# The heads' space in two pools, the first freed one head early, and the gates' token sums made in the last head

## The chip, the core and the metric

The kernel runs on one core of one Trainium2 chip. The metric is the device time of one execution in microseconds (us): the median of three executions before the change is 1059.69 us, the lowest 1058.46 us and the highest 1060.88 us. The engines are named as the profile names them: PE is TensorE (matrix products; PEld is its weight load), DVE is VectorE, ACT is ScalarE, POOL is GpSimd and SP is SyncE. SP issues the loads of the weights, POOL the transfers between the steps of the heads.

## The reference, cut to what matters

One decoder layer over 256 tokens (S) of width 2048 (D_MODEL), everything in float32. All four gate and channel products are slices of one projection `proj`:

```python
h = _rmsnorm(x, pre_norm_g)
proj = jnp.einsum('bsd,de->bse', h, w_in)
(q_a, c_kv, k_rope, z_mla, c_in, b_gate, c_gate, z_conv, g_mla, g_conv) = jnp.split(proj, cuts, axis=-1)
...
attn = _causal_mla_attention(q_nope, q_rope, k_nope, k_rope, v)
attn = attn.reshape(b, s, MLA_WIDTH) * jax.nn.silu(z_mla)
y_mla = jnp.einsum('bse,ed->bsd', attn, w_o_mla)
u = c_gate * c_in
u_pad = jnp.pad(u, ((0, 0), (CONV_K - 1, 0), (0, 0)))
conv = sum(conv_w[k] * u_pad[:, k:k + s] for k in range(CONV_K))
y_conv = jnp.einsum('bse,ed->bsd', b_gate * conv * jax.nn.silu(z_conv), w_o_conv)
merged = jax.nn.sigmoid(g_mla) * y_mla + jax.nn.sigmoid(g_conv) * y_conv
out = jnp.einsum('bsd,de->bse', merged, w_out)
x = x + _rmsnorm(out, post_norm_g)
```

There are 16 heads. `g_mla` and `g_conv` are the gates whose "token sums" the change moves.

## The kernel before

**Exact products from split halves.** Every float32 operand is split into a high part in the reduced format fp32r and a low part, the rest; a product is three matmuls (high by high, high by low, low by high) into one PSUM bank (`product`). A weight comes in units of 1 MB, numbered in one plan. SP loads unit n into a buffer `raw`, ACT copies it into `whi` (the high part) and DVE subtracts, `wlo = raw - whi` (`split_act`, line 262). There are three buffers each of `raw`, `whi` and `wlo`: unit n+3 is loaded into the buffer of unit n once both engines have split that unit, and is split into the buffers of unit n once PE has read them. `ahead` issues three loads ahead and splits one unit ahead of the one in use.

**Stages.** First the latent projections, then a loop over 16 heads, then four gate blocks (two gates, two halves of the width), then the two square projections and the output projection. In the loop every head h has four channel units (`channels(h, 0)` to `channels(h, 3)`: a quarter of the contraction each, into two banks `cv`), between which stand the scores of the head, `turn` (the softmax weights of the head before it, turned through DRAM: DVE writes `via`, POOL stores it to `far` and loads it back as `p`, ACT and DVE split it into `pt`) and `values` (their product with V, in the bank `o`). The scores of head 15 are made in head 14 already. The units of head 14 are 105 to 108, those of head 15 are 109 to 112. `channels_done` empties the two `cv` banks (`cv_w`, line 726). Every fourth head the gated convolution is made on DVE and POOL (`taps`: three shifted copies `mv` of `cv_f`, each multiplied by a row `cw` of the convolution's weights, which POOL loads, line 743; DVE's products are line 759). The last one, for t = 0, is issued at the end of head 14 and its products are made in head 15.

**The gate blocks.** Of the 16 blocks of a gate's contraction six are taken in three pairs with a scheme of seven products instead of eight, which needs sums of weights (`split_pair`, lines 204 to 220: `tf` from `raw`, `raw` changed in place, `thi` and `tlo` the halves of `tf`) and sums of tokens (`token_sums`, lines 891 to 906: from `x_both`, sums `xf`, then four tiles `xsf`, split into `xs`). The eight banks of a gate block are those that the heads used: two of tag `cv`, one `o`, one `st`, four `mm`. The first gate block begins with unit 113, a plain unit (four banks: `cv`, `st`, `cv`, `o`, in this order); then come unit 114, a pair, 115, plain, 116, a pair, and so on by turns. Only pairs need `xs`, `tf`, `thi` and `tlo`, of which there is one buffer each.

**Memory.** `bp` is the pool of the loop over heads: the latent tiles `qa`, `ckv` and `kr`, the mask, and all temporary tiles (`temp`, line 326). It is closed after the last head (line 867), and `sg` (the gates' results) and `d1` (the gate blocks' tiles, with `xs`, `tf`, `thi`, `tlo`) are opened behind it, in the space that it leaves. So the first tile of `d1` can be written once the last transfer or instruction that reads the tiles of `bp` at that place is done.

**What sets the order.** A scheduler puts the instructions of ACT, DVE, POOL and SP into the order of each engine's queue when the program is built; matmuls and the calls marked `keep_in_program_order` stay in the order of the code. Each queue is then worked off in that order: an instruction that waits holds all behind it.

Of the kernel before, what the change touches and what calls it, by code (L numbers as in the profile page):

```python
# [11 lines left out]
F32 = mybir.dt.float32  # L12
F32R = mybir.dt.float32r
I32 = mybir.dt.int32
AF = mybir.ActivationFunctionType
ALU = mybir.AluOpType
PSUM = bass.MemoryType.PSUM

P = 128
S = 256  # L20
NT = S // P
D = 2048
KD = D // P
H = 16
# [4 lines left out]
KR = R // P  # L29
# [9 lines left out]
LINE = 32  # L39
# [3 lines left out]
PAIRS = 3  # L43
STEP = 4
# [40 lines left out]
def tile_layer(ctx: ExitStack, tc: tile.TileContext, xw, x, pos, pvec, post_g, wc, wz, wcv, wkr, wqk, wqr, wv, cwr, wsq, wg, out):  # L85
    nc = tc.nc
# [36 lines left out]
    for h in range(H):  # L123
        g, second = divmod(h, HG)
# [176 lines left out]
    main = ctx.enter_context(ExitStack())  # L301
# [5 lines left out]
    cv_f = fp.tile([P, KD, S], F32, name="cv_f")  # L307
    bstack = main.enter_context(ExitStack())
    bp = bstack.enter_context(tc.tile_pool(name="bp", bufs=1, side="right"))
    qa = bp.tile([P, KR, 2 * S], F32R, name="qa")  # L310
    ckv = bp.tile([P, KR, 2 * S], F32R, name="ckv")
    kr = bp.tile([P, 2, S], F32R, name="kr")
    mask = bp.tile([P, 3 * P], F32, name="mask")
    nc.gpsimd.memset(mask[:, :], 0.0)
    for o in (0, 2 * P):
        make_causal_mask(nc, mask[:, o : o + P], mask_val=MASKED)
# [9 lines left out]
    def temp(name, shape=(P, S), dt=F32, bufs=2, tag=None):  # L326

        tag, n = tag or name.rstrip("0123456789_"), shape[-1]
        if n % LINE == 0:
            return bp.tile(list(shape), dt, name=name, tag=tag, bufs=bufs)  # L330
        return bp.tile([P, -(-n // LINE) * LINE], dt, name=name, tag=tag, bufs=bufs)[:, :n]


    def turned(src, via, n):
# [402 lines left out]
    def taps(j, t):  # L737
# [31 lines left out]
        join(u, u, parts[0], ALU.add)  # L769
        yield  # L770

    cv_w = bp.tile([P, NT, 512], F32, name="cv_w")
    tap, coming, ps_by_head = None, [], {}

# [3 lines left out]
    def score(h):  # L778
        ps_by_head[h], come = scores(h)
        coming.append(come)  # L780

    for h in range(H):
        v, at = divmod(h, HV)

        if at == 0:
            for i in range(4):
                if v == 0 and i == 1:

                    def turn_keys():
                        latent_turn("ckv", ckv, "kv_g", (("mm", 4), ("mm", 4)))  # L790
                        next(table_parts)

                    gates(v, i, turn_keys)
                else:
                    gates(v, i)
                if v == 0 and i == 0:
                    latent_turn("qa", qa, "q_g", (("st", 1), ("o", 1)))
                elif v == 0 and i == 2:
                    key_rope()
                elif v and i == 0:  # L800
                    arrive()
                    pt = turn(ps_by_head.pop(h - 1))
                elif v and i == 1:
                    values(h - 1, pt)
                    make("v", v)
                    next(tap)
                elif v and i == 2:
                    next(tap)
            gates_done(v)
        if h == 0:  # L810
            for i in first:
                make(*i)
            channels(h, 0)
        if h < H - 1:
            score(h)
        if h:
            channels(h, 0)
        if at == 0:
            coming.append(gates_turn(v, 0))
        else:  # L820
            pt = turn(ps_by_head.pop(h - 1))
        channels(h, 1)
        if at == 0:
            arrive()
            coming.append(gates_turn(v, 1))
        else:
            values(h - 1, pt)
        if h == H - 2:
            score(h + 1)

        if at == 2 or h == H - 1:
            next(tap)
        if at and h < H - 1:
            arrive()
        channels(h, 2)
        if at == 0:
            arrive()
            if v:
                coming.append(channels_join(v - 1, 0))
        if at == 2 or h == H - 1:  # L840
            next(tap)
        for i in made[h]:
            make(*i)
        if h == H - 1:
            pt = turn(ps_by_head.pop(h))
        channels(h, 3)
        if at == 0:
            while coming:
                arrive()
        if h == H - 2:  # L850
            arrive()
        if h == H - 1:
            values(h, pt)
        if at == 3:
            coming.append(channels_join(v, 1))
        if at == 1:
            tap = taps(v, 1)
            next(tap)
        elif at == 3 and h + 1 < H or h == H - 2:
            tap = taps(v, 0)  # L860
            next(tap)
# [3 lines left out]


    bstack.close()
    sgp = main.enter_context(tc.tile_pool(name="sgp", bufs=1))
    sg = sgp.tile([P, 2, NT, D], F32, name="sg")
    dstack = main.enter_context(ExitStack())  # L870
    d1 = dstack.enter_context(tc.tile_pool(name="d1", bufs=1))
    at_both = m_both = x_both

    def split_turned(src, both, c, t):
# [9 lines left out]
    def split_channels(i):  # L884

        j, t = divmod(i, NT)
        split_turned(cv_t[:, j, t, :], cv_both, j, t)

    xs = d1.tile([P, 4, PAIRS, 2, P], F32R, name="xs")

    def token_sums():


        both = x_both[:, :, :].bitcast(F32).rearrange("p (g k) c -> p g k c", k=STEP)[:, :2, :PAIRS]
        xf = d1.tile([P, 2, PAIRS, S], F32, name="xf", tag="tf", bufs=1)
        s = d1.tile([P, 4, PAIRS, P], F32, name="xsf", tag="thi", bufs=1)
        tt = nc.vector.tensor_tensor
        for g in range(2):
            tt(xf[:, g], both[:, g, :, :S], both[:, g, :, S:], op=ALU.add)
        a = [[xf[:, g, :, t * P : (t + 1) * P] for g in range(2)] for t in range(NT)]  # L900
        tt(s[:, 0], a[1][0], a[1][1], op=ALU.add)
        tt(s[:, 1], s[:, 0], a[0][0], op=ALU.subtract)
        tt(s[:, 2], a[0][0], a[1][0], op=ALU.subtract)
        tt(s[:, 3], a[0][1], s[:, 1], op=ALU.subtract)
        for i in range(4):
            split_act(xs[:, i, :, 0], xs[:, i, :, 1], s[:, i])

    def side(n, j):

# [11 lines left out]
    def gate_block(n, b, last):  # L921


        units, kinds = u_g[2 * n + b], gate_kinds()[n, b]
        ps = {m: bank(f"g{n}{b}_{m}", *TAGS[m]) for m in TAGS}
        begun = set()
        ends = {}
        for i, (kind, _) in enumerate(kinds):
            for m in TAGS if kind == "pair" else ():
                ends[m] = i  # L930
            for m in (2, 3, 4, 0) if kind == "whole" else ():
                ends[m] = i
        last_pair = max(i for i, (kind, _) in enumerate(kinds) if kind == "pair")

        def add_to(m, a, w, i, end):
            product(ps[m][:, :], a, w, m not in begun, end and ends[m] == i)
            begun.add(m)

        for i, (kind, ks) in enumerate(kinds):
            if last:  # L940
                for v in {6: (0, 1), 7: (2,)}.get(i, ()):
                    split_branch(v)
            if n == b == i == 0:
                token_sums()
            w = take(units[i])
            if kind == "pair":
                for m in TAGS:
                    if m:
                        add_to(m, side(m, ks[0]), w[m], i, True)
            else:  # L950
                for m, t, half in ((2, 0, 0), (3, 0, 1), (4, 1, 0), (0, 1, 1)):
                    for j, k in enumerate(ks):
                        a = [x_both[:, k, o + t * P : o + (t + 1) * P] for o in (0, S)]
                        add_to(m, a, w(2 * j + half, 512), i, j == len(ks) - 1)
            if i == last_pair:
                p1, p5 = wide("p1"), wide("p5")
                u = d1.tile([P, 3, 512], F32, name="u", tag="u", bufs=1)
                nc.scalar.activation(p1[:, :], ps[1][:, :], AF.Copy)
                nc.scalar.activation(p5[:, :], ps[5][:, :], AF.Copy)
                tt = nc.vector.tensor_tensor  # L960
                tt(u[:, 0], ps[6][:, :], p1[:, :], op=ALU.add)
                tt(u[:, 2], ps[7][:, :], u[:, 0], op=ALU.add)
                tt(u[:, :2], u[:, 0::2], p5[:, :].rearrange("p (o c) -> p o c", o=1).to_broadcast([P, 2, 512]), op=ALU.subtract)
        for m, t, half, other in ((2, 0, 0, p1[:, :]), (3, 0, 1, u[:, 0]), (4, 1, 0, u[:, 2]), (0, 1, 1, u[:, 1])):
            o = 1024 * b + 512 * half
            g = sg[:, n, t, o : o + 512]
            tt(g, ps[m][:, :], other, op=ALU.add)
            nc.scalar.activation(g, g, AF.Sigmoid, scale=r_col[:, t : t + 1])
# [30 lines left out]

    for c in range(4):  # L1000
        pss = tokens(c, 0, at_both)
        if c == 1:
            fstack.close()
        for t, m in enumerate(merged(0, c)):
            nc.vector.tensor_tensor(m, pss[t][:, :], m, op=ALU.mult)
    waiting = None
# [201 lines left out]
```

## Time and profile before

| | |
|---|---|
| median of three executions | 1059.69 us |
| the profiled execution's own time | 1061.09 us |
| its span in the profile | 1059.3 us |
| PE busy, share of the span | 1024.0 us, 97% |
| DVE busy | 742.5 us, 70% |
| ACT busy | 532.5 us, 50% |
| POOL busy | 180.3 us, 17% |
| mean granted clock of PE | 0.988 |

The profile is one execution with the hardware's own times. Its page gives the busy time of each engine, the span in 40 slices of 26.5 us, the chain of work that ended last (followed back from the last instruction, at each step to what released it) and the costliest groups of instructions. Further views list instructions in order of time, waits by what ended them, and busy time in chosen stretches. In a row of the timeline stand the start, the time (of all of "x2" together), the engine, the line, the operation, output and input tiles, and in brackets the idle time of the engine before it with what ended it. The span is 1.8 us shorter than the profiled execution's time, which is 1.4 us above the median.

### The profile page before, as it was taken

What the parts mean: (1) busy time and instruction counts of PE and PEld (TensorE: products, weight loads), DVE (VectorE), ACT (ScalarE), POOL (GpSimd) and SP (SyncE); (2) the same over time, 40 slices, a digit from 0 to 9 for tenths busy, and PEclk for the clock granted to TensorE, in tenths of its full rate; (3) what the DMA queues carried; (4) which work ended last, traced back from release to release, by engine and by line L of the source; (5) the groups of instructions that cost most, each with busy time, mean ns of one, the idle gap of its engine ahead of it and who ended that gap; (6) DMA issues with size and microseconds to landing.
All of it is one profiled execution on the core that took longest, in us unless ns stands there. A gap on an engine that the chain in (4) does not pass through costs nothing.

```text
span 1059.3 us, 12469 instructions
## 1 busy us (share of the span) xinstructions
PE 1024.0 (97%) x4658; PEld 851.8 (80%) x4658; DVE 742.5 (70%) x960; ACT 532.5 (50%) x675; POOL 180.3 (17%) x345
## 2 busy tenths in 40 slices
PE   9999999999999999999999839999999999999997
PEld 8887888888878888788888728888888888888885
DVE  7578769686687777777677579797976445666462
ACT  7756546455465455455555145555565333334451
POOL 7621220204202042112422210000000000232000
PEclk9999999999999999999999969999999999999999
DMA  8754766667666685656767536655555555677842
GB/s 339 299 188 176 254 221 210 219 222 277 193 230 214 214 296 182 232 208 238 267 230 231 173 113 203 216 200 214 186 211 198 194 187 186 238 250 252 321 159 79
DMA packets 41948, 231.00 MB, mean 218 GB/s; under 512 B 7520, under 2 KB 8224, under 8 KB 18976
## 3 DMA queue, kind: packets, MB, share of 16 engines
q1 hardware_dynamic: 29808, 197.54, 52.4%
q0 software_dynamic: 11648, 29.38, 9.2%
q10 hardware_dynamic: 432, 3.29, 0.7%
q8 instruction: 36, 0.59, 0.2%
q14 instruction: 24, 0.20, 0.0%
HBM read 214.48 MB, written 11.53 MB: 213 GB/s over the span
## 4 chain that ended last, share of the span: by engine, by line
PE 90%; DVE 4%; issue 2%; DMA 2%; ACT 1%; POOL 1%; DVEq 0%; POOLq 0%
PE cv L90 28%; PE sq L90 16%; PE g L90 15%; PE z L90 8%; PE out L90 8%; PE qa L90 2%; PE qn L90 2%; PE ckv L90 2%; PE kn L90 2%; DMA cw<-cwr_dram 2%; PE vv L90 2%; PE sc L90 1%; DVE wlo L264 1%; ACT whi L263 1%; PE o L90 1%
## 5 line engine op out<-in xcount | busy, mean ns | idle before, releaser
L264 DVE TENSOR_TENSOR wlo<-raw,whi 128x1024 fp32r<-128x1024 f32 (+2 forms) x290 | 423.4, 1484 | 224.7 <-ACT whi L263 223.8
L263 ACT ACTIVATE whi<-raw 128x1024 fp32r<-128x1024 f32 (+2 forms) x292 | 357.5, 1259 | 380.3 <-issue 120.5
L90 PE MATMUL cv<-whi,x_both 128*128 128x512 f32 x1024 | 323.4, 390 | 3.3 <-DVE cv_w L726 3.3
L90 PEld LDWEIGHTS cv<-whi,x_both 128*128 128x128 f32 x1024 | 192.3, 188 | 43.5 <-DVE cv_w L726 4.3
L90 PE MATMUL cv<-wlo,x_both 128*128 128x512 f32 x512 | 199.7, 390 | 0.0
L90 PE MATMUL g<-whi,x_both 128*128 128x512 f32 x368 | 119.8, 390 | 0.0
L90 PEld LDWEIGHTS cv<-wlo,x_both 128*128 128x128 f32 x512 | 96.2, 188 | 18.7
L90 PEld LDWEIGHTS g<-whi,x_both 128*128 128x128 f32 x368 | 69.4, 189 | 14.4
L90 PE MATMUL z<-whi,x_both 128*128 128x512 f32 x256 | 80.6, 390 | 0.0
L90 PE MATMUL sq<-whi,x_both 128*128 128x512 f32 x256 | 79.0, 389 | 0.0
L90 PE MATMUL sq<-whi,cv_both 128*128 128x512 f32 x256 | 78.9, 389 | 0.0
L90 PE MATMUL out<-whi,x_both 128*128 128x512 f32 x256 | 78.9, 389 | 0.0
L345 POOL DMA_DIRECT2D far<-sg x32 | 17.5, 553 | 330.4 <-DVE sg L1014 287.8
L345 POOL DMA_DIRECT2D far<-via x64 | 35.3, 559 | 225.2 <-DVE via L338 224.2
L90 PE MATMUL g<-wlo,x_both 128*128 128x512 f32 x184 | 71.8, 390 | 0.0
L90 PEld LDWEIGHTS z<-whi,x_both 128*128 128x128 f32 x256 | 48.1, 188 | 9.9
L90 PEld LDWEIGHTS sq<-whi,cv_both 128*128 128x128 f32 x256 | 48.0, 188 | 9.9
L90 PEld LDWEIGHTS out<-whi,x_both 128*128 128x128 f32 x256 | 48.0, 188 | 9.9
L90 PEld LDWEIGHTS sq<-whi,x_both 128*128 128x128 f32 x256 | 48.0, 188 | 9.9
L90 PE MATMUL z<-wlo,x_both 128*128 128x512 f32 x128 | 49.8, 389 | 0.0
L90 PE MATMUL sq<-wlo,x_both 128*128 128x512 f32 x128 | 49.8, 389 | 0.0
L90 PE MATMUL sq<-wlo,cv_both 128*128 128x512 f32 x128 | 49.8, 389 | 0.0
(243 smaller groups left out, 1325.3 us busy)
## 6 DMA issues: line engine op xcount, KB each, us to landing
raw<-wcv_dram SPq DMA_DIRECT2D x64, 1024.0 KB, 5.1
raw<-wsq_dram SPq DMA_DIRECT2D x48, 1024.0 KB, 4.8
raw<-wg_dram SPq DMA_DIRECT2D x32, 1024.0 KB, 4.8
raw<-wz_dram SPq DMA_DIRECT2D x16, 1024.0 KB, 4.8
raw<-wqk_dram SPq DMA_DIRECT2D x8, 1024.0 KB, 5.6
cw<-cwr_dram POOLq DMA_DIRECT2D x24, 256.0 KB, 7.2
raw<-wc_dram SPq DMA_DIRECT2D x4, 1024.0 KB, 9.9
raw<-wv_dram SPq DMA_DIRECT2D x4, 1024.0 KB, 5.6
```

What stands on the lines that cost most here:

```text
L90: return tc.keep_in_program_order(nc.tensor.matmul(*a, **kw))
L263: a = nc.scalar.activation(hi, src, AF.Copy)
L264: b = nc.vector.tensor_tensor(lo, src, hi.bitcast(F32), op=ALU.subtract)
L345: tc.keep_in_program_order(nc.gpsimd.dma_start(out=f[i], in_=m))
```

## The change

The pool `bp` becomes two. `ep` stands behind it on the same side and takes `qa`, `ckv`, `kr`, the mask and those temporary tiles whose tags belong to the norms, the rotary tables, the queries and the keys; `bp` keeps the rest (`p`, `via`, `pt`, `f`, `cw`, `mv`, V). `ep` is closed in head 14, after the scores of head 15 are issued, and `d1` with `xs` is opened there, in its space and in what was free beside it. `token_sums` is called in head 15 after `channels(15, 2)`, behind the `turn` of head 15, which moves up ahead of the second step of the convolution, instead of in the first gate block. `sg` moves to the side where `bp` was; the space of `at_f` and `cv_f` is no longer released in the first square projection. The instructions are the same ones, 4,647 matmuls in the same order, and the queues of POOL and SP hold the same DMAs in the same order; DVE's and ACT's queues are ordered anew around heads 14 and 15.

```diff
-    qa = bp.tile([P, KR, 2 * S], F32R, name="qa")
...
+    estack = main.enter_context(ExitStack())
+    ep = estack.enter_context(tc.tile_pool(name="ep", bufs=1, side="right"))
+    qa = ep.tile([P, KR, 2 * S], F32R, name="qa")
+    ckv = ep.tile([P, KR, 2 * S], F32R, name="ckv")
+    kr = ep.tile([P, 2, S], F32R, name="kr")
+    mask = ep.tile([P, 3 * P], F32, name="mask")
...
+        pool = ep if tag.startswith(("rms_", "ta_", "rp_", "qn_", "kn", "qr")) else bp
...
+    def token_sums(d1, xs):
+        both = x_both[:, :, :].bitcast(F32).rearrange("p (g k) c -> p g k c", k=STEP)[:, :2, :PAIRS]
+        xf = d1.tile([P, 2, PAIRS, S], F32, name="xf", tag="tf", bufs=1)
+        s = d1.tile([P, 4, PAIRS, P], F32, name="xsf", tag="thi", bufs=1)
...
+    dstack = main.enter_context(ExitStack())
+    def sums_space():
+        estack.close()
+        d1 = dstack.enter_context(tc.tile_pool(name="d1", bufs=1))
+        return d1, d1.tile([P, 4, PAIRS, 2, P], F32R, name="xs")
...
         if h == H - 2:
             score(h + 1)
+            d1, xs = sums_space()
...
+        if h == H - 1:
+            pt = turn(ps_by_head.pop(h))
+            token_sums(d1, xs)
         if at == 2 or h == H - 1:
             next(tap)
         for i in made[h]:
             make(*i)
-        if h == H - 1:
-            pt = turn(ps_by_head.pop(h))
...
-    sgp = main.enter_context(tc.tile_pool(name="sgp", bufs=1))
+    sgp = main.enter_context(tc.tile_pool(name="sgp", bufs=1, side="right"))
...
-            if n == b == i == 0:
-                token_sums()
...
-        if c == 1:
-            fstack.close()
```

Three places of DVE's queue show what moved (line numbers are those of the kernel that a row belongs to; a tile's first number, as in `wlo110`, is the unit's or the head's). The first is the softmax of head 15, issued in head 14, up to the turn of its weights (`via_5067` before, `via_5070` now). `mx`, `nb` and `rs` are its row maxima, their negatives and the reciprocal sums; `wlo110` is the low half of unit 110; `cv_w` empties the banks of head 14. Before the change:

```order
L633 TENSOR_REDUCE mx_5055<-p_5049 128x1 x2
L634 TENSOR_SCALAR nb_5058<-mx_5055 128x2
L641 RECIPROCAL rs_5057<-sm_5056 128x2
L644 TENSOR_SCALAR p_5049<-p_5049,rs_5057 128x128
L644 TENSOR_SCALAR p_5049<-p_5049,rs_5057 128x256
L338 STREAM_TRANSPOSE via_5067<-p_5049 128x3x4x32
L759 TENSOR_TENSOR mv1_4917<-mv1_4917,cw_4923 128x512
L759 TENSOR_TENSOR mv2_4920<-mv2_4920,cw_4925 128x512
L264 TENSOR_TENSOR wlo110_5166<-raw110_5114,whi110_5165 128x1024 x2
```

and after it, where `xf` (two instructions), `nb` and two of the four `xsf` stand just ahead of these rows, between `mx` and the first of them:

```order
L264 TENSOR_TENSOR wlo110_5174<-raw110_5122,whi110_5173 128x1024
L786 TENSOR_TENSOR xsf_5289<-xsf_5289,xf_5288 128x384
L264 TENSOR_TENSOR wlo110_5174<-raw110_5122,whi110_5173 128x1024
L644 RECIPROCAL rs_5060<-sm_5059 128x2
L788 TENSOR_TENSOR xsf_5289<-xf_5288,xsf_5289 128x384
L264 TENSOR_TENSOR xs_5081<-xsf_5289,xs_5081 128x3x128 x2
L729 SCALAR_TENSOR_TENSOR cv_w_617<-cv14_0_4964,r_both_105,cv_w_617 128x512
L647 TENSOR_SCALAR p_5052<-p_5052,rs_5060 128x128
L647 TENSOR_SCALAR p_5052<-p_5052,rs_5060 128x256
L264 TENSOR_TENSOR xs_5081<-xsf_5289,xs_5081 128x3x128 x2
L729 SCALAR_TENSOR_TENSOR cv_w_617<-cv14_1_4965,r_both_105,cv_w_617 128x512
L341 STREAM_TRANSPOSE via_5070<-p_5052 128x3x4x32
```

The token sums (`xf`, `xsf`, `xs`), unit 110 and both `cv_w` of head 14 now stand ahead of `via`; before, unit 110 and the two `cv_w` stood behind it and the sums from 29 rows behind it on.

The second place is the split weights of head 14 (`pt_5195` before, `pt_5203` now), for which PE's products of head 14 wait; they stand in PE's queue between the units 110 and 111. `tf114`, `raw114` and `tlo114` belong to the first pair of the gates, unit 114. Before:

```order
L264 TENSOR_TENSOR wlo111_5201<-raw111_5163,whi111_5200 128x1024 x2
L759 TENSOR_TENSOR cv_f_114<-cv_f_114,cw_5077 128x512
L759 TENSOR_TENSOR cv_f_114<-cv_f_114,mv1_4917 128x512
L264 TENSOR_TENSOR pt_5195<-p_4936,pt_5195 128x384
L264 TENSOR_TENSOR wlo112_5248<-raw112_5198,whi112_5247 128x1024 x2
L264 TENSOR_TENSOR wlo113_5285<-raw113_5245,whi113_5284 128x2048
L412 TENSOR_TENSOR f_5235<-o14_5230,half_5236 128x256
```

and after:

```order
L264 TENSOR_TENSOR wlo112_5256<-raw112_5206,whi112_5255 128x1024 x2
L210 TENSOR_TENSOR tf114_5383<-raw114_5306 128x1024
L762 TENSOR_TENSOR cv_f_114<-cv_f_114,cw_5085 128x512
L211 TENSOR_TENSOR raw114_5306<-raw114_5306,tf114_5383 128x512
L762 TENSOR_TENSOR cv_f_114<-cv_f_114,mv1_4920 128x512
L212 TENSOR_TENSOR tf114_5383<-raw114_5306 128x512
L264 TENSOR_TENSOR wlo113_5309<-raw113_5253,whi113_5308 128x2048
L264 TENSOR_TENSOR pt_5203<-p_4939,pt_5203 128x384
L264 TENSOR_TENSOR tlo114_5385<-tf114_5383,thi114_5384 128x1536
L415 TENSOR_TENSOR f_5243<-o14_5238,half_5244 128x256
L264 TENSOR_TENSOR pt_5285<-p_5052,pt_5285 128x384
```

The weight sums of unit 114, which stood behind the token sums at the end of the loop, and the split of unit 113 moved ahead of `pt` of head 14; before, that `pt` stood ahead of the units 112 and 113.

The third place is the last step of the convolution in head 15 and the emptying of the first bank of head 15's channels (`cv_w<-cv15_0`), into which the first gate block's first product is written. Before:

```order
L759 TENSOR_TENSOR mv1_5151<-mv1_5151,cw_5157 128x512
L759 TENSOR_TENSOR mv2_5154<-mv2_5154,cw_5159 128x512
L759 TENSOR_TENSOR mv1_5151<-mv1_5151,mv2_5154 128x512
L726 SCALAR_TENSOR_TENSOR cv_w_614<-cv15_0_5161,r_both_105,cv_w_614 128x512
L759 TENSOR_TENSOR cv_f_114<-cv_f_114,cw_5243 128x512
L759 TENSOR_TENSOR cv_f_114<-cv_f_114,mv1_5151 128x512
L264 TENSOR_TENSOR pt_5279<-p_5049,pt_5279 128x384
L730 TENSOR_TENSOR cv_f_114<-cv_f_114,cv_w_614 128x512
L726 SCALAR_TENSOR_TENSOR cv_w_614<-cv15_1_5162,r_both_105,cv_w_614 128x512
```

and after:

```order
L674 TENSOR_TENSOR at_f_113<-f_5243,at_f_113 128x8x32
L210 TENSOR_TENSOR tf116_5448<-raw116_5417 128x1024
L762 TENSOR_TENSOR mv1_5159<-mv1_5159,cw_5165 128x512
L211 TENSOR_TENSOR raw116_5417<-raw116_5417,tf116_5448 128x512
L762 TENSOR_TENSOR mv2_5162<-mv2_5162,cw_5167 128x512
L212 TENSOR_TENSOR tf116_5448<-raw116_5417 128x512
L762 TENSOR_TENSOR mv1_5159<-mv1_5159,mv2_5162 128x512
L762 TENSOR_TENSOR cv_f_114<-cv_f_114,cw_5251 128x512
L762 TENSOR_TENSOR cv_f_114<-cv_f_114,mv1_5159 128x512
L264 TENSOR_TENSOR wlo114_5382<-raw114_5306,whi114_5381 128x2048
L729 SCALAR_TENSOR_TENSOR cv_w_617<-cv15_0_5169,r_both_105,cv_w_617 128x512
```

The emptying of the bank stood ahead of the products that wait for the last row of the convolution's weights (`cw_5243`); now it stands behind them (`cw_5251`), behind the weight sums of the second pair (unit 116) and behind the low half of unit 114. `pt` of head 15, which stood behind these products, went ahead of them (it is in the second place's rows, `pt_5285`).

## The prediction on record

> **What bounds the kernel now.** First the page: who is busy, and where that breaks off.
>
> ```profile
> PE 1024.0 (97%) x4658; PEld 851.8 (80%) x4658; DVE 742.5 (70%) x960; ACT 532.5 (50%) x675; POOL 180.3 (17%) x345
> PEclk9999999999999999999999969999999999999999
> ```
>
> PE is busy for 97% of the span, and its granted clock, in tenths for 40 slices of 26.5 us, sags in one place, slice 24 (609 to 636 us). So only what shortens or makes waits of PE counts. PE's waits, by what ended them:
>
> ```profile
> PE g L90 <- ACT thi L263: 16.5, 1, 16.5
> PE o L90 <- DVE pt L264: 2.6, 1, 2.6
> PE g L90 <- DVE tlo L264: 2.2, 1, 2.2
> ```
>
> Two of the three are in the first gate block (`g`), ahead of its first pair. The chain that ended last says what stood in front of them:
>
> ```profile
> 610.39 1.95 DMA far<-mv
> 612.52 1.82 DVE xf L899 x2
> ...
> 619.99 1.92 ACT whi L263
> ...
> 626.34 1.76 DVE tlo L264
> 628.14 162.30 PE g L90 x707
> ```
>
> The last transfer out of the heads' space lands at 612.3, then come the token sums (`xf` on), the weight sums, the halves `thi` and `tlo`, and from 628.14 PE runs without a break to its end. The clock shows in short stretches and in PE's timeline (behind the engines' busy times stand the granted clock, the DMA share and GB/s):
>
> ```profile
> 600.00:604.00 4.00, 1.65 (x9) 1.46 (x10) 3.65 (x6) 0.38 (x1) 0.00 (x0) 1.00 0.02 4
> 612.00:614.00 2.00, 0.00 (x0) 0.00 (x0) 1.48 (x2) 0.00 (x0) 0.55 (x1) 0.50 0.44 131
> 630.00:632.00 2.00, 2.00 (x6) 1.58 (x5) 0.77 (x2) 1.84 (x1) 0.00 (x0) 0.53 0.46 188
> 608.25 0.39 PE L90 MATMUL g<-whi,x_both 128*128 128x512 f32 x1
> 632.03 0.40 PE L90 MATMUL g<-wlo,xs 128*128 128x512 f32 x1
> 565.73 10.92 PE cv L90 x48
> ```
>
> A matmul takes 10.92 / 48 = 0.2275 us. PE stops at 608.6, the clock is half by 612 (0.50), and half until just before 632 (0.53 from 630 to 632): from 628.1 that is 3.7 us of work at half speed, a loss of 1.9. The 2.6 us of waiting for `pt`, between 600 and 604, cost no clock (1.00). The matmul of 632.03 is the eleventh of unit 114, so at full speed the unit would have begun at 632.03 - 10 x 0.2275 = **629.76**. This is the mark that the change has to beat: behind it PE waits for nothing.
>
> **The change, part by part.** The sums leave this place whole; that alone would free PE. But DVE's queue shows three new things ahead of what PE waits for, so I follow that queue from the row maxima of head 15 (`mx`, 569.07 + 0.60).
>
> *The turn of head 15 comes later.* These rows give the durations:
>
> ```profile
> 568.87 0.28 DVE L627 TENSOR_TENSOR p<-p,mask 128x128 f32<-128x128 f32 x1
> 569.07 0.60 DVE L633 TENSOR_REDUCE mx<-p 128x1 f32<-128x256 f32 x2
> 571.72 0.58 DVE L338 STREAM_TRANSPOSE via<-p 128x384 f32<-128x384 f32 x1
> 615.31 0.56 DVE L902 TENSOR_TENSOR xsf<-xsf,xf 128x384 f32<-128x384 f32 x1
> 615.79 1.02 DVE L264 TENSOR_TENSOR xs<-xsf,xs 128x384 fp32r<-128x384 f32 x2
> 573.39 2.35 DVE L264 TENSOR_TENSOR wlo<-raw,whi 128x1024 fp32r<-128x1024 f32 x2
> 577.40 0.75 DVE L726 SCALAR_TENSOR_TENSOR cv_w<-cv,r_both,cv_w 128x512 f32<-128x512 f32 x1 [0.39 <-ACT cv_w L723]
> 570.94 0.17 DVE L641 RECIPROCAL rs<-sm 128x2 f32<-128x2 f32 x1 [1.05 <-ACT p L637]
> 577.07 0.50 PE L90 MATMUL cv<-whi,x_both 128*128 128x512 f32 x1 [0.43 <-DVE cv_w L726]
> 580.32 0.53 ACT L263 ACTIVATE pt<-p 128x384 fp32r<-128x384 f32 x1 [1.06 <-DMA p<-far]
> ```
>
> Ahead of `via` now stand `xf` 1.8, four `xsf` 2.2, four `xs` 2.1, unit 110 2.35 and two `cv_w` 1.5, together 10.0; neighbours overlap by some 0.08 (-0.9), and the 1.05 of idleness before `rs` is filled. So `via` begins 8.0 later, at 579.7. Of these, `xf`, the `xsf`, unit 110 and two `xs` stand ahead of the first `cv_w` too (7.8 with `nb` and `rs`, less 0.7): DVE reaches it at 576.8 and is done near 577.7, so unit 109, which waits for the bank, starts some 0.7 later than at 577.07, and units 109 and 110 end at 577.8 + 10.92 = 588.7. The turned `p` of head 14 comes 8.6 us behind `via` (580.32 - 571.72), now at 588.3; it is not the last thing there.
>
> *Unit 114 is loaded later, and PE's head 14 waits for it.* Behind `via` and two products `mv`, unit 111 is split (0.5 + 1.2 + 2.35) by 583.8, and the load into its buffer, that of unit 114, is issued at 583.9:
>
> ```profile
> 575.78 0.33 SPq L161 DMA_DIRECT2D raw<-wg_dram  x1
> ...
> raw<-wg_dram SPq DMA_DIRECT2D x1, 1024.0 KB, 9.7
> ...
> raw<-wg_dram SPq DMA_DIRECT2D x1, 1024.0 KB, 7.2
> ...
> raw<-wg_dram SPq DMA_DIRECT2D x1, 1024.0 KB, 8.9
> ...
> raw<-wg_dram SPq DMA_DIRECT2D x32, 1024.0 KB, 4.8
> 588.09 0.39 PE L90 MATMUL o<-pt,vv_hi 128*128 128x512 f32 x1
> 564.22 0.57 PE o L90 x4
> 617.66 1.22 DVE L210 TENSOR_TENSOR tf<-raw 128x1024 f32<-128x1024 f32 x1
> 580.62 0.69 DVE L759 TENSOR_TENSOR cv_f<-cv_f,cw 128x512 f32<-128x512 f32 x1
> 590.23 2.29 DVE L264 TENSOR_TENSOR wlo<-raw,whi 128x2048 fp32r<-128x2048 f32 x1 [3.89 <-ACT whi L263]
> 581.95 0.55 DVE L264 TENSOR_TENSOR pt<-p,pt 128x384 fp32r<-128x384 f32 x1
> ```
>
> Unit 114's load took 9.7 us before, beside `mv` and `cw`; unit 113's, issued 4.1 after `via` began (575.78) and so in the company that unit 114 has now (583.9, 4.2 after `via`), 7.2; unit 115's 8.9; the median is 4.8. I take 7.2: landed at 591.1. DVE then makes `tf`, `cv_f`, `raw`, `cv_f`, `tf` (1.22 and four of 0.69), `wlo113` (2.29) and only then `pt` of head 14 (0.55): 6.8 less 0.5 of overlap. PE's head 14, which ran unhindered at 588.09, starts at **597.5**, after 8.8 us of waiting.
>
> [...]
>
> *PE from there.* 8.8 us of idleness halve the clock again (1.9 lost): head 14's product 0.57, units 111 and 112 10.95, 1.9, head 15's product 0.57: PE is through at 611.5. Head 15's `pt` now comes early, so the 2.6 us wait goes.
>
> *The last row of the convolution is late.* The first gate product needs a `cv` bank, emptied by `cv_w`, and that now stands behind `tf` of unit 116 and behind the convolution.
>
> ```profile
> 584.11 1.09 POOL L743 DMA_DIRECT2D cw<-cwr_dram  x2
> 594.22 0.69 DVE L759 TENSOR_TENSOR mv<-mv,cw 128x512 f32<-128x512 f32 x1 [0.90 <-DMA cw<-cwr_dram]
> 600.32 0.69 DVE L759 TENSOR_TENSOR cv_f<-cv_f,cw 128x512 f32<-128x512 f32 x1 [2.51 <-DMA cw<-cwr_dram]
> ```
>
> `wlo113` ends at 597.0 and frees the buffer for unit 116; its load runs beside two `cw`, as unit 115's did, whose 8.9 us I take (bounds 4.8 and 9.7 as before): 605.9. `tf116` ends at 607.1. The two `cw` are loaded behind `cv_f` (done at 594.1; before, 580.62 and two of 0.69, at 582.0); the first ended the wait at 594.22, 12.2 later, which now is 606.3: just in time. From the first `mv` product to the product with the last row passed 600.32 - 594.22 = 6.1, one `cw` load: 607.0 to 613.1. Two `cv_f` (1.4), `wlo114` (2.29) and `cv_w` (0.75) less overlap: 4.2. PE begins the gates at **617.3**, having waited 5.8.
>
> *The rest.* Unit 113's 24 matmuls take 5.45; the clock costs 1.9 once more: unit 114 begins at **624.65**. Its `tlo`, `xs` and weights are long there. The last quarter of unit 113 needs the bank `o`, emptied some 5.0 after the first `cv_w` (622.3), before PE is there (623.3).
>
> *Sum.* 629.76 - 624.65 = 5.1 us gained. As a check: waits of 16.5, 2.6 and 2.2 go, 0.7, 8.8 and 5.8 come, and half-clock work costs 1.9 more: 4.1; the missing 1.0 is idleness beside the records that the waits do not count. The profiled execution took 1061.1 (its span 1059.3 and 1.8 around it), so 1056.0; it was 1.4 above the median, so from 1059.7: **1054.6**. Two other edits cost nothing: `sg` at another place is written only after the gates, and the later release of `at_f` frees nothing that a later tile asks for before PE's last products.
>
> [...]
>
> **The rivals.**
>
> *The whole wait goes.* If `pt` of head 14 and `cv_w` were not held back, PE would run from 588.7 through 0.57 + 10.92 + 0.57 + 5.45 to 606.2: 23.6 gained, 1036. For it: the waits named in the profile all belong to the moved work. Against: both rows stand where the queue shows them, behind loads. Chance 0.05.
>
> *Quick loads.* With 4.8 for units 114 and 116 and for `cw`, head 14 starts at 595.1, PE is through at 609.1, `cv_w` ends at 610.6; a wait of 1.5 keeps the clock, and unit 114 begins at 617.0 (0.9 of waiting for `o`): 12.8 gained, **1046.9**. Against: five transfers share those microseconds. Chance 0.15.
>
> *Slower: the loads in series decide.* Everything after 583.9 hangs on the loads of 114 and 116 one after the other, because DVE's queue puts `tf114` ahead of `pt` and `tf116` ahead of the convolution. Each microsecond of either is one of the result. Together 16.1 in my sum; above 16.1 + 5.1 = 21.2 it is slower than before, at 11.7 each 1061.9. For it: 9.7 occurred. Against: two of 9.7 still give 1057.9. Chance 0.08 to be slower by over 0.2%.
>
> *The change doesn't do what it says*: `xf` finds the space still taken and waits as before, about 1059.7. The queue shows `xf` right behind `mx`, and the space's last reader, the mask of head 15 on DVE (the scores on PE come before it), ends at 569.15. Chance 0.02.
>
> **How the numbers follow.** My forecast, loads between the extremes, has 0.70 and gives 1054.6. Its ends are those of the unknown loads, 1046.9 (4.8 each) and 1057.9 (9.7 each); the range 1047 to 1058 leaves out the whole gap and the slower case. 0.2% is 2.1 us, about what a measurement can tell from no change. Faster by more: 0.84 (whole, quick, and the forecast but for its upper end); within: 0.08; slower: 0.08.
>
> **What would show it.** PE's waits should name `pt` before the product of head 14 (8 to 9 us, near 589 to 597) and `cv_w` before the gates (5 to 6 us), and no wait on `thi`; the clock should be half twice. `via` of head 15 should begin near 580, and `xf` near 569.6 without waiting. It is wrong if PE's head 14 does not wait, if the loads of 114 and 116 take under 5 or over 10 us, or if a wait appears later in the gates.

## The result and the profile after

| | before | after |
|---|---|---|
| median (four executions of each) | 1059.45 us | 1054.36 us |
| lowest to highest | 1058.46 to 1060.88 | 1053.15 to 1054.72 |
| the profiled execution, and its span | 1061.09, 1059.3 | 1054.07, 1052.3 |
| mean granted clock of PE | 0.988 | 0.992 |

The ratio is 0.9949, with a 95% interval of 0.9932 to 0.9966: half a per cent faster. The two spans are 7.0 us apart and the medians 5.1, because the profiled execution of before was 1.6 above the median of its four and that of after 0.3 below.

The waits of PE in the profile after, by what ended them (total, times, longest):

```profile
PE o L90 <- DVE pt L264: 8.6, 1, 8.6
PE cv L90 <- DVE cv_w L729: 3.9, 4, 1.2
PE g L90 <- DVE cv_w L729: 3.7, 1, 3.7
```

The waits of before (`thi` 16.5, `pt` of head 15 2.6, `tlo` 2.2) are gone. Two new ones stand for them, the first row (`pt` of head 14) and the third (`cv_w` ahead of the gates); the second was there before with 3.3. What made the new ones shows in the chain of work that ended last, from the load of unit 114 on (start, time, what):

```profile
583.03 7.38 DMA raw<-wg_dram
590.41 0.02 issue
590.44 1.23 DVE tf L210
...
594.07 2.21 DVE wlo L264
596.28 0.02 issue
596.30 9.02 DMA raw<-wg_dram
605.32 0.02 issue
605.34 0.07 DVE tf L210
605.41 1.08 issue
606.49 0.69 DVE mv L762
607.18 0.28 issue
607.47 3.74 DMA cw<-cwr_dram
611.21 0.02 issue
611.23 0.70 DVE cv_f L762
...
612.65 2.20 DVE wlo L264
614.85 0.67 DVE cv_w L729
615.52 0.04 issue
615.57 9.63 PE g L90 x34
```

Three transfers in series take 20.1 of the 32.5 us, with DVE's work between them. The timelines of DVE and PE show who stood behind (in brackets the idle time of the engine before the row, and what ended it):

```profile
568.35 0.61 DVE L636 TENSOR_REDUCE mx<-p 128x1 f32<-128x256 f32 x2
568.87 1.82 DVE L783 TENSOR_TENSOR xf<-x_both 128x768 f32<-128x768 f32 x2
578.98 0.57 DVE L341 STREAM_TRANSPOSE via<-p 128x384 f32<-128x384 f32 x1
590.44 1.23 DVE L210 TENSOR_TENSOR tf<-raw 128x1024 f32<-128x1024 f32 x1 [4.09 <-DMA raw<-wg_dram]
596.19 0.55 DVE L264 TENSOR_TENSOR pt<-p,pt 128x384 fp32r<-128x384 f32 x1
596.89 0.77 PE L90 MATMUL o<-pt,vv_hi 128*128 128x512 f32 x1 [8.64 <-DVE pt L264]
615.57 0.50 PE L90 MATMUL g<-whi,x_both 128*128 128x512 f32 x1 [3.69 <-DVE cv_w L729]
622.76 0.39 PE L90 MATMUL g<-thi,xs 128*128 128x512 f32 x1
```

`xf` starts without a wait in the freed space. DVE stands 4.1 us for unit 114's load with `pt` of head 14 queued behind `tf`, and PE waits 8.6 for that `pt`. Unit 114 begins at 622.76. All of this execution is 0.72 earlier than before's already ahead of the change (`mx` at 568.35, 569.07 before), so in the prediction's numbering unit 114 begins at 623.48, where 624.65 was forecast and the mark was 629.76.

### The profile page after: what moved, and what is told of

It is laid out like the page before. It is cut to its first block, busy times and chain, and to the rows that moved or that the text cites. A ratio compares the mean times of both kernels' runs of the same rounds, so it can differ in the third digit from the quotient of the medians.

```text
span 1052.3 us, 12469 instructions
## 1 busy us (share of the span) xinstructions
PE 1025.4 (97%) x4658; PEld 853.2 (81%) x4658; DVE 741.3 (70%) x960; ACT 531.8 (51%) x675; POOL 180.8 (17%) x345
## 4 chain that ended last, share of the span: by engine, by line
PE 88%; DVE 5%; DMA 3%; issue 3%; ACT 1%; POOL 0%; DVEq 0%; POOLq 0%; ACTq 0%
PE cv L90 26%; PE sq L90 17%; PE g L90 16%; PE z L90 8%; PE out L90 8%; PE qa L90 2%; PE qn L90 2%; DVE wlo L264 2%; PE ckv L90 2%; PE kn L90 2%; PE vv L90 2%; DMA raw<-wg_dram 2%; DMA cw<-cwr_dram 1%; PE sc L90 1%; PE qr L90 1%
```

## The experiments

Each run is the changed kernel with some places on DVE's queue altered; no_last_tap leaves out a load instead. "Behind" is an order between two instructions of one engine, with no semaphore and no data: `behind(a, b)` below queues a after b. The scheduler keeps this order and chooses the places of the other instructions anew. The code below is cut to what matters. Ratios are to the kernel before, run on the same chip, with 95% intervals; the medians of before beside the runs lay between 1058.8 and 1060.1 us, so medians of different runs compare to about 1 us:

| run | PE's wait for `pt` of head 14 | wait of the gates for `cv_w` | median, us | ratio |
|---|---|---|---|---|
| the change | 8.6 | 3.7 | 1054.36 | 0.9949 (0.9932 to 0.9966) |
| sums_late | none | none (`thi` 10.5, `tlo` 2.2) | 1052.89 | 0.9939 (0.9924 to 0.9953) |
| pt_first | 4.9 | 1.6 | 1046.90 | 0.9880 (0.9863 to 0.9896) |
| cvw_first | 8.6 | 0.5 | 1051.21 | 0.9922 (0.9907 to 0.9936) |
| both_first | 4.9 | 0.6 | 1047.05 | 0.9884 (0.9868 to 0.9899) |
| no_last_tap | 8.7 | 2.7 | 1051.91 | 0.9928 (0.9912 to 0.9945) |
| via_first | none | none | 1039.01 | 0.9810 (0.9796 to 0.9823) |
| via_pt_behind | 2.0 | 1.6 | 1042.79 | 0.9849 (0.9835 to 0.9862) |
| via_cvw_first | none | none | 1040.32 | 0.9823 (0.9810 to 0.9837) |
| cvw14_first | none | 0.5 | 1039.83 | 0.9815 (0.9800 to 0.9829) |

**sums_late: the space, with the sums late.**

```
-            token_sums(d1, xs)              # in the last head
...
+            if n == b == i == 0:            # in the first gate block
+                token_sums(d1, xs)
...
+    behind(xf, second cv_w of head 15)
```

> The changed kernel with all its pools, but the token sums traced in the first gate block and queued on VectorE behind the last cv_w of head 15, where the kernel before had them. Theory (the place of the sums on VectorE's queue is the gain): the wait of the first gate products for thi, 16.5 us in the kernel before, comes back, no wait of 8 us stands before the products of head 14, and the time is that of the kernel before, 1058 to 1062 us. Rival (the pools, the side of sg or the place of the call bring it): the time stays at 1054.4 us.

The theory fell on the time and on the 16.5 us wait; the rival's time, 1054.4, is nearer. The sums are back behind the last `cv_w`, and yet the run is 7.2 us faster than before and no slower than the change. DVE's timeline:

```profile
600.96 0.74 DVE L729 SCALAR_TENSOR_TENSOR cv_w<-cv,r_both,cv_w 128x512 f32<-128x512 f32 x1
601.62 1.81 DVE L783 TENSOR_TENSOR xf<-x_both 128x768 f32<-128x768 f32 x2
```

`xf` follows `cv_w` at once. Among DVE's waits in the profile of before stands, for the same instruction:

```profile
DVE xf L899 <- DMA far<-mv: 6.6, 1, 6.6
```

So DVE stood 6.6 us for the last transfer out of the old space. With the space free PE waits 10.5 us ahead of the products with `thi` in place of 16.5, 6.0 less:

```profile
L90 PE MATMUL g<-thi,xs 128*128 128x512 f32 x8 | 3.8, 526 | 10.5 <-issue 10.5
```

(the last column is the idle time ahead of the group; "issue" is a wait whose end the profile pins on nothing; ACT, which makes `thi`, is busy to 616.5, and PE, which stopped at 606.1, starts 10.5 later, at 616.6). The space is not all of the 7.2: the run also keeps the change's earlier `turn` of head 15, whose `pt` DVE makes at 591.49, and the 2.6 us wait for it is gone, while one of 1.0 for `f` came. The change takes the 10.5 away too, and pays 8.6 + 3.7 of new waits for it: the early sums, as the scheduler queues them, bring nothing that can be measured.

**pt_first and cvw_first: one order each.** In `split_pair`, for the three operations of `tf`:

```
+    behind(tf of unit 114, pt of head 15)               # pt_first
+    behind(tf of unit 116, second cv_w of head 15)      # cvw_first
```

> The changed kernel with the three operations of unit 114's tf queued on VectorE behind pt of head 14, and nothing else. Theory (TensorE's wait for pt is VectorE standing at tf for load 114, in front of pt): pt then stands only behind two tap products (their weights landed at 586.4 us in the changed kernel) and wlo of unit 113 (its whi ended at 590.2): 590.3 + 2.3 + 0.55 and 0.1 give 593.3, so the wait falls from 8.6 to about 5.2 us; the moving and the loads behind it come 3 to 4 us earlier too, the wait of the gates goes to about 2.5 us, and the time is about 1047 us (1045 to 1051). Rival (the wait comes from the probabilities' own way, whose via stands 8 us later behind the sums, wherever tf stands): the wait stays 8.6 us and the time 1054.4 us.

> The changed kernel with the three operations of unit 116's tf queued on VectorE behind the last cv_w of head 15, and nothing else. Theory (the gates' wait is VectorE standing at tf for load 116, and what then follows in series up to cv_w): the wait for pt stays 8.6 us; the tap products run when their weights land, about 604.1 in place of 606.5, and lose the two tf operations between them, so the gates' wait falls from 3.7 to about 1.7 us; a later wait of up to 2.4 us may come in the gates. The time is about 1051 us (1050 to 1053). Rival (the last load of tap weights and wlo of unit 114 set it): the wait stays 3.7 us and the time 1054.4 us.

The first order reaches further than its expectation says. When the program splits unit 114, the newest `pt` is already that of head 15, so `tf` is queued behind the `pt` of both heads. Head 14's wait is the same either way, since nothing of `tf` stands ahead of its `pt`; what the later place of `tf` does to the rest was not tried.

Both times came out as forecast: 1046.90 for 1047, 1051.21 for 1051. The gain of cvw_first over the change is small beside the noise (their intervals overlap). DVE in pt_first:

```profile
590.23 2.29 DVE L264 TENSOR_TENSOR wlo<-raw,whi 128x2048 fp32r<-128x2048 f32 x1 [1.60 <-ACT whi L263]
592.44 0.55 DVE L264 TENSOR_TENSOR pt<-p,pt 128x384 fp32r<-128x384 f32 x1
595.88 1.22 DVE L210 TENSOR_TENSOR tf<-raw 128x1024 f32<-128x1024 f32 x1
```

`pt` is 3.7 us earlier than in the change (596.19) and its wait shrinks by 3.7 to 4.9. The run gains 7.5, twice that: the load of unit 116, the tap products and `cv_w` hang on the same queue and come earlier too (the load is issued at 592.55, not 596.30; the first `mv` product starts at 598.68, not 606.49; `cv_w` at 608.56, not 614.76), and the clock is half for a shorter time (0.50 from 592 to 598; the mean granted clock is 0.995, in the change 0.992).

The 4.9 us that stay are an order too. In the change and in pt_first, `pt` of head 14 is queued behind the split of unit 113, on DVE (`wlo` above) and on ACT alike. ACT in the change (0.04 earlier in pt_first):

```profile
588.33 1.91 ACT L263 ACTIVATE whi<-raw 128x2048 fp32r<-128x2048 f32 x1 [3.43 <-issue]
590.14 0.51 ACT L263 ACTIVATE pt<-p 128x384 fp32r<-128x384 f32 x1
```

Unit 113 is split into the buffers of unit 110, which PE reads last before it turns to head 14, at 588.25; so `whi` cannot begin earlier, and `whi` 1.91, `wlo` 2.29 and `pt` 0.55 are 4.75 of the 4.9. The turned `p` of head 14 was there: in the change its load was issued at 582.56 and landed 4.9 us later, at 587.5.

In cvw_first the tap products start when their weights land,

```profile
602.26 0.69 DVE L762 TENSOR_TENSOR mv<-mv,cw 128x512 f32<-128x512 f32 x1 [2.17 <-DMA cw<-cwr_dram]
610.62 0.75 DVE L729 SCALAR_TENSOR_TENSOR cv_w<-cv,r_both,cv_w 128x512 f32<-128x512 f32 x1
```

and `cv_w` is at 610.62 in place of 614.76; 1.9 of the wait comes back later in the gates (`PE g` on DVE's `f`).

**both_first.**

> The changed kernel with both of these orders: tf of unit 114 behind pt of head 14, tf of unit 116 behind the last cv_w of head 15. Theory: waits of 5.2 us for pt and about 1 us for cv_w, and one of up to 2.5 us in the gates; about 1046.5 us (1044 to 1051). If the two gains simply added up, it would be 1044. Rival (one of the two waits takes the place of the other's): no less than the better of the two single orders less 0.5 us.

1047.05, no better than pt_first: with `pt` early, the order of unit 116 only moves a wait, from `cv_w` (1.6 to 0.6) to `f` later in the gates (0.6 to 1.9). The gains of the two (7.5 and 3.2) overlap almost wholly.

**no_last_tap: one transfer of the series.**

```
-        cw = tap(0)
+        cw = cws[1] if (j, t) == (3, 0) else tap(0)
```

> The changed kernel without the last load of tap weights in head 15 (one of 256 KB): the last tap product takes weights that are there already, so a part of the computation is changed. It prices the term that the prediction had at 6.1 us (from the first tap product to the last join) and the profile has at 4.7. Theory (tf of unit 116 and this load stand in series in front of cv_w): the joins follow the tap products at once, wlo of unit 114 starts near 610.8 in place of 612.6 and the gates' wait falls from 3.7 to about 2 us; time 1051 to 1053 us. Rival (load 116 alone sets the wait): the wait stays 3.7 us, the time 1054.4.

Without that load the kernel computes something else, so the run only prices the load. The wait falls by 1.0 to 2.7 (expected 2.0; `wlo` of unit 114 starts at 611.04, not 610.8). The median is 2.4 lower, though the intervals of the two ratios overlap. The load is a part of the gates' wait, not the whole.

**via_first: the sums in the last head, but behind the softmax.** In `token_sums`:

```
+    behind(xf, via of head 15)
```

> The changed kernel with xf, the first of the token sums, queued on VectorE behind via of head 15 (the sums stay in head 15, in the freed space); the scheduler then puts pt of head 14 ahead of tf of unit 114 by itself. The run with the sums late, 1052.9, has already shown that freeing the space gives 7 us without any sum in head 15, and that the early sums are worth nothing as the changed kernel queues them. Theory (what the early sums win is given back because they hold up via, and because tf stands for load 114 in front of pt): via is at 570 again, pt of head 14 near 584, TensorE does not wait for it; in the gates 1 to 3 us of waits remain; time about 1042 us (1039 to 1046). Rival (the DMA loads of units 114 and 116 set the time, wherever via stands): TensorE waits 4 us or more at the head's end and the time is not under 1047, what the better order of pt alone gave.

1039.01, 3 us below the forecast's middle and at the edge of its range, and 15 below the change. DVE's timeline:

```profile
571.19 0.58 DVE L341 STREAM_TRANSPOSE via<-p 128x384 f32<-128x384 f32 x1
573.99 1.82 DVE L783 TENSOR_TENSOR xf<-x_both 128x768 f32<-128x768 f32 x2
584.00 0.56 DVE L264 TENSOR_TENSOR pt<-p,pt 128x384 fp32r<-128x384 f32 x1
589.12 1.22 DVE L210 TENSOR_TENSOR tf<-raw 128x1024 f32<-128x1024 f32 x1
601.57 0.74 DVE L729 SCALAR_TENSOR_TENSOR cv_w<-cv,r_both,cv_w 128x512 f32<-128x512 f32 x1
```

`via` is 7.8 earlier than in the change, `pt` 12.2, `cv_w` 13.2. Neither new wait is left; behind the head PE's longest is 0.6. The rival (the loads set the time) falls: the same loads are made.

**via_pt_behind: which of the two made the wait.**

```
+    behind(xf, via of head 15)
+    behind(pt of head 14, tf of unit 114)
```

> The kernel of the run via_first with one order put back: pt of head 14 queued on VectorE behind the last operation of unit 114's tf, as in the changed kernel, while via stays early. Theory (the place of tf alone makes TensorE's wait for pt): load 114 lands about 590.3, the three tf operations end near 593, and the wait for pt is back with 4 to 5 us although the probabilities have long landed; time about 1047 us (1044 to 1050). Rival (only the late via made that wait): no wait for pt, and the time of the run via_first.

The wait is back, so the place of `tf` alone makes one; but it is 2.0 us, not 4 to 5, and the run 4 us better than expected. DVE did not stand for the load this time:

```profile
587.40 1.23 DVE L210 TENSOR_TENSOR tf<-raw 128x1024 f32<-128x1024 f32 x1
590.34 0.55 DVE L264 TENSOR_TENSOR pt<-p,pt 128x384 fp32r<-128x384 f32 x1
```

`tf` starts with no idle time before it. (The list of waits names ACT's `whi` for the 2.0 us; they end at 591.0, 0.1 behind DVE's `pt`.) Unit 114's load was issued 1.3 us earlier (581.70, not 583.03) and took 5.2 instead of 7.4.

This does not part the wait cleanly into a share of the late `via` and a share of `tf`. In pt_first `via` is late and `tf` stands behind, and 4.9 us are left, but there the split of unit 113 stands ahead of `pt`, and here behind it. What the runs show is the queue. With `via` late, the wait is 8.6 where `tf` and unit 113 stand ahead of `pt`, and 4.9 where unit 113 does alone; with `via` early, it is 2.0 where `tf` stands ahead (it did not stand for its load), and none where neither does. By its data alone the late `via` would cost little, as an estimate: `p` landed at 587.5, and 0.51 on ACT and 0.55 on DVE make 588.5, against 588.25, when PE is ready. No run has `via` late and `pt` ahead of unit 113, and why the scheduler put it behind where `via` is late is not shown.

**via_cvw_first and cvw14_first: is more to be had?** The first adds `behind(tf of unit 116, second cv_w of head 15)` to via_first; the second puts `xf` behind the second `cv_w` of head 14 instead of behind `via`.

> The kernel of the run via_first with tf of unit 116 queued behind the last cv_w of head 15 besides. Theory: the tap products and cv_w lose the stand for load 116, but it was hardly in their way any more, so between 0 and 1.5 us less than the run via_first. Rival (the order of tf 116 is worth as much as in the changed kernel): 3 us less than via_first.

> The changed kernel with xf, the first of the token sums, queued on VectorE behind the second cv_w of head 14 (and so behind via of head 15, which is ahead of it). In the run via_first TensorE still waited 2.2 us for cv_w at 576 (1.1 in the kernel before), for xf and one half of wlo stood ahead of it, and one half-clock stretch of 3.4 us followed that wait in the profiled execution. Theory: that wait is 1.1 us again and the half clock does not follow it, 1 to 2.7 us less than via_first: 1036.5 to 1038 us. Rival (the sums, now later, press on what VectorE does for the gates, and the wait comes back there): 1039 us or more.

Neither is faster than via_first (1040.32 and 1039.83; all three intervals overlap), so both forecasts of a further gain missed. In cvw14_first the wait for `cv_w` at 576 did go from 2.2 to 0.4, but small waits came back for the gates (0.9, 0.7 and 0.5 in its list), as the rival said. No version run is clearly better than via_first, 1.9% faster than before.

## Why the prediction was right, and where its sizes were off

The two new waits stand where the prediction put them, for the reason it gave: loads and splits ahead of `pt` and `cv_w` on DVE's queue. Its time agrees to 0.2 us, closer than its terms, which were off by up to 1.4 us in both directions and cancelled in part.

- **`via` 8.0 later.** Shown: 578.98 + 0.72 = 579.70, forecast 579.7. It was not the arrival of `p` that this held up too long, as the prediction said ("it is not the last thing there").
- **Load of 114 issued at 583.9, 7.2 us; head 14 waits 8.8.** Issued at 583.75 in the same numbering, 7.4 us; the wait is 8.6. That the queue held `pt`, and not the arrival of `p`, shows in `p`'s landing at 587.5 and in pt_first. The prediction had `wlo113` in its sum as one item of 2.29; it did not see that with unit 113's split ahead of `pt`, PE would wait 4.9 us even without `tf`.
- **The clock.** The first half-clock stretch was worth more than the 1.9 forecast: from 596.89, the product of head 14, to 611.88 (615.57 less its 3.69) PE took 15.0 us where the sum had 14.0. The second, 3.4 us at half speed, cost 1.7. That a pause of 5.8 us loses the clock was the author's estimate: before lists no wait of PE between 2.6 and 16.5 us. The change shows it behind 8.6 us (0.50 from 594 to 602) and behind 3.7 (0.59 and 0.56 from 616 to 620).
- **Load of 116, 8.9.** It took 9.02.
- **From the first `mv` product to the last join, 6.1.** This is the term that was mis-sized: 611.23 - 606.49 = 4.7, because that `cw` load took 3.74, where the one in the row it was read from (600.32 - 594.22) took 5.1. A weight load was under way beside that one (issued at 592.55) and none beside this one (the one ahead had landed at 605.32, the next was issued at 614.88); that this made the difference is the author's estimate and was not tried alone. no_last_tap shows that the transfer counts.
- **The gates' wait, 5.8.** 3.7: PE came 1.1 later (611.88 + 0.72 against 611.5, the clock), and the gates began 1.0 earlier (615.57 + 0.72 against 617.3, the `cw` load).
- **Unit 114 at 624.65.** At 623.48. In these two executions the change was therefore worth 6.3 us and not 5.1; that the medians give 5.1 exactly is partly luck.
- **"The sums leave this place whole; that alone would free PE."** True, but it hid a second cause. sums_late shows that 6 us of the 16.5 go when the space alone is free. The prediction quoted the transfer that ended at 612.3 and did not price it by itself, and so did not see that the same time could be had without moving a single sum.
- **The rivals.** The whole wait going (1036) was given 0.05 as an outcome of this queue, and it did not happen; via_first reaches 1039.0 by one order on the same work. Quick loads (1046.9) did not come true for units 114 and 116, only for the last `cw`. The slower case needed 21.2 us of the two loads; they took 16.4.

## What to carry to other kernels

Where work is moved into a busier place, read what its instructions stand ahead of on their own engine's queue: here the same change, with the sums placed 5 us later behind one turn of the softmax, was worth 20 us where it had been worth 5, and 7 of the 20 came without moving any sum. An instruction that waits stops everything behind it, whether it waits for a load (`tf`, 4.1 us) or, like unit 113's split, for PE to finish with a buffer: there PE came to need `pt`, which stood behind the split, and waited 4.9 us. Put such an instruction behind whatever is ready and waited for elsewhere. Where a long wait ends with the release of a buffer, price the release and the work behind it apart: one may be had without the other.

## What the hardware showed that was not expected

The prediction went by the length of a pause: the 2.6 us of before had kept the clock (1.00 from 600 to 604), and it had pauses of 8.8 and 5.8 lose it. It is not the length alone. In the profiled execution of via_first (1040.69 us, the slowest of its five) a pause of 2.17 us was followed by half a clock; in via_cvw_first the same pause was not. First via_first, then via_cvw_first (PE's first row after the pause; then stretches, with the granted clock behind the busy times, ahead of the DMA share and GB/s):

```profile
578.27 0.50 PE L90 MATMUL cv<-whi,x_both 128*128 128x512 f32 x1 [2.17 <-DVE cv_w L729]
578.00:580.00 2.00, 1.73 (x7) 1.39 (x8) 2.00 (x5) 1.96 (x4) 0.00 (x0) 0.89 0.77 279
580.00:582.00 2.00, 2.00 (x6) 1.60 (x5) 2.00 (x3) 0.12 (x1) 0.00 (x0) 0.50 0.65 242
582.00:584.00 2.00, 2.00 (x8) 1.54 (x7) 2.00 (x5) 0.53 (x1) 0.00 (x0) 0.75 0.44 135
```

```profile
577.78 0.50 PE L90 MATMUL cv<-whi,x_both 128*128 128x512 f32 x1 [2.17 <-DVE cv_w L729]
578.00:580.00 2.00, 2.00 (x10) 1.61 (x10) 2.00 (x4) 1.59 (x4) 0.00 (x0) 1.00 0.69 258
580.00:582.00 2.00, 2.00 (x10) 1.66 (x9) 2.00 (x3) 0.00 (x0) 0.00 (x0) 1.00 0.48 188
```

In via_first the clock is half from about 579.6 (0.89 of 2 us) to 583.0 (0.75 of 2 us), some 3.4 us, and the drop comes 1.3 us after PE had started again; these times are an estimate from the granted clock of the stretches, taken as either full or half. In the profile after:

```profile
592.00:594.00 2.00, 0.00 (x0) 0.00 (x0) 2.00 (x5) 0.00 (x0) 0.47 (x2) 0.61 0.02 8
602.00:604.00 2.00, 2.00 (x9) 1.64 (x8) 0.00 (x0) 0.00 (x0) 0.00 (x0) 0.83 0.60 244
616.00:618.00 2.00, 2.00 (x7) 1.61 (x6) 2.00 (x4) 0.00 (x0) 0.00 (x0) 0.59 0.83 299
618.00:620.00 2.00, 2.00 (x6) 1.53 (x5) 2.00 (x2) 0.00 (x0) 0.00 (x0) 0.56 0.46 193
```

the stretches run, by the same reckoning, from 592.4 to 602.7 and from 616.4 to 619.8, 10.2 and 3.4 us, the second again beginning 0.8 after PE's start at 615.57; the two drops are 23.9 us apart. The second stretch is as long as that of via_first, the first three times as long, and the distance seven times.

In via_first PE was idle from 576.1 to 578.3; in via_cvw_first it was idle from 575.6 to 577.8, and the granted clock stayed 1.00 to 584. Why the one pause cost the clock and the other did not is not shown, and how much idleness is needed was not tried.

One and the same load does not always take the same time: unit 114's took 7.4 us in the change and 5.2 in via_pt_behind, issued 1.3 us earlier. In the change it ran beside the two loads of `p`, issued at 582.56 and 583.95 and landed 4.9 and 6.7 us later; in via_pt_behind, where `via` is 8.2 earlier, both had landed near 580.2 (an estimate: the second issued 5.0 behind `via`, as in the change, and the 4.5 that it took). That this is the reason was not tried alone.
